# Five paddings that place float32r matmul operands 128 bytes apart modulo 256

## The chip, the cores and the metric

The kernel runs on one core of a Trainium2 chip. The metric is the device time of one launch in microseconds (us), lower is better. Tiles live in SBUF, the on-chip memory of 128 partitions; an address here is a byte offset within a partition. Matmuls run on TensorE (PE): the stationary operand is loaded by a weight load (PEld) and the moving operand streams past it into PSUM, the accumulation memory. The other engines are VectorE (DVE), ScalarE (ACT), GpSimd (POOL) and SyncE (SP), which issues the DMA transfers.

## The reference

Two blocks follow each other on 256 tokens of width 1024, all in float32. Cut to what matters here:

```python
# first block: layer 0 = window attention + S5 scan (with a GLU), layer 1 = attention over selected keys
for layer in range(2):
    hn = rms_norm(h, norm_g[layer])
    h = h + (even_layer if layer == 0 else odd_layer)(hn, ...)   # products with w_in, w_out, glu_w
# second block: layer 0 = attention, layer 1 = chunked SSM, both with 256 context tokens
for i in range(2):
    h, hc = modulate(x, ...), modulate(ctx, ...)
    y, yc = attention_mixer(h, hc, ...) if i == 0 else ssm_mixer(h, hc, ...)
    x = x + g1 * y
    x = x + g2 * swiglu(modulate(x, ...), w_gate[i], w_up[i], w_down[i])   # width 2816
    # the context gets the same in layer 0
return rmsnorm(x, final_norm_g)
```

Most of the work are products of 256 tokens with weight matrices: 1024 x 2304, 1024 x 3144, 1024 x 1536, 1024 x 6208, the three feed-forward matrices of each layer, and the output products.

## The kernel before

**Products.** Each weight tile of 128 x 1024 is fetched by one DMA into `raw`; `Weights.load` (L173) has ACT write its rounded copy `h` as float32r (L179) and DVE the remainder `l` (L180). Activations are split in the same way into a high and a low tile (`nhx` and `nlx`, `fh` and `fl`, `yH` and `yL` and so on). A product is the sum of three float32r matmuls: high by high, low by high, high by low. All go through the helper `mm` (L129), so all have line L130; in the profile `out<-moving,stationary` names their tiles. There are two forms:

- `feat_tiles` (L273) has the weights stationary and the activations moving, 256 columns. The output has features on partitions. Feed-forward gate and up (`pffnx`, `pffnc`), the SSM's projections (`pcvx`), gates (`pg`), the GLU (`pglu`) and others use it: for every k first `h` with the high and with the low activation, then, after all k, `l` with the high one.
- `tok_step` (L231) has the activations stationary (128 tokens) and the weights moving, 256 or 512 columns. The output has tokens on partitions (`pdx` for x, `pdc` for the context).

Every matmul has a weight load of its own, also where the stationary operand is the same as before. The weight load for the next matmul runs while the present one streams.

**Order.** The program is traced by a scheduler; the x chain and the context chain share TensorE. The last stages are x alone: the SSM's output product (stationary `ysH`, `ysL`), then the feed-forward of layer 1 in two halves of 11 column tiles, each with its product back to width 1024.

**Addresses.** Pools on the left are stacked upwards from the bottom of the partition in the order in which they are opened, those with `right=True` downwards from the top; a tile lies right behind the one before it. Left: `con` (constants, first tile `pad`, L110), `res`, `act` (split activations), `wk`, `xw`, then the stages' own pools (`ev`, `evat`, `od`, `l0`, `ff0`, `l1`, `ff1`). Right: `padr` (L189), `wx` (x weights), `wc` (context weights, L191), `cx` (context tiles, L192). Tiles that hold matmul operands have sizes that are multiples of 256 bytes, as have the slices of 128, 256 or 512 columns that a matmul takes, so each keeps one residue modulo 256: `h` and `l` of both weight pools 192; everything in `act` 0; `fh` and `fl` 0, in `cx` and in `ff0` and `ff1`; the GLU's `glH`, `glL` 192; `QxT`, `KxH`, `KxL` (L1220 and L1221) 0; `ysH`, `ysL` 128. The other places of the change are `sink` (L596, in `evat`, ahead of `glH` and `glL`) and `d_row` (L1332, in `l1`, ahead of `ysH` and `ysL`).

Of the kernel before, what the change touches and what calls it, by code (L numbers as in the profile page):

```python
# [8 lines left out]
F32 = mybir.dt.float32  # L9
# [79 lines left out]
def build(tc, A):  # L89
# [5 lines left out]
    def D(name):  # L95
        return A[name]

    def dram(a, off, ap):
        return bass.AP(tensor=a.tensor, offset=a.offset + off, ap=ap)

    def pool(name, bufs=1, space=None, right=False):
        kw = {"side": "right"} if right else {}
        if space is not None:
            kw["space"] = space
        else:
            kw["reuse_waits"] = "tile"
        return tc.tile_pool(name=name, bufs=bufs, **kw)

    con = es.enter_context(pool("con"))
    con.tile([128, 8], F32, name="pad")  # L110
    res = es.enter_context(pool("res"))
    act = es.enter_context(pool("act"))
    wk = es.enter_context(pool("wk", 2))
# [15 lines left out]
    def mm(out, l, r, start, stop, mark=None):  # L129
        i = T.matmul(out, l, r, start=start, stop=stop)  # L130
        if mark is not None:
            marks.setdefault(mark, i.ins)
# [55 lines left out]
    cst = ExitStack()  # L188
    es.enter_context(pool("pr", right=True)).tile([128, 8], F32, name="padr")  # L189
    wx = Weights("x", *WX, SY, es)  # L190
    wc = Weights("c", *WC, SY, cst)  # L191
    cx = cst.enter_context(pool("cx", right=True))  # L192
    xw = es.enter_context(pool("xw"))
    xpool = {"x": (xw, "xn"), "c": (cx, "cfl")}
# [31 lines left out]
    def w_plain(a, ncols):  # L226
        def src(k0, nk, n0, n):
            return [(lambda t: t, dram(a, k0 * 128 * ncols + n0, [[ncols, 128], [128 * ncols, nk], [1, n]]))]
        return src
# [16 lines left out]
    def dense_tok(w, src, actk, kt, chunks, evac, ps, tags="ddd", last=None):  # L246
        for ci, (n0, n) in enumerate(chunks):
            pt = [ps.tile([128, 512], F32, tag=tags[ci], name=f"pd{ps.k}{m}") for m in range(2)]
            kstep = 1024 // n
            for k0 in range(0, kt, kstep):  # L250
                ks = range(k0, min(k0 + kstep, kt))
                wh, wl = w.load(src(k0, len(ks), n0, n), len(ks), n)
                tok_step(pt, wh, wl, ks, n, actk, kt, last if ci == len(chunks) - 1 else None)
            for m in range(2):
                evac(ci, m, pt[m][:, :n], n0)
# [176 lines left out]
    def even_layer(hook):  # L432
        with ExitStack() as st:
            p = st.enter_context(pool("ev"))
# [6 lines left out]
            uT = p.tile([128, 4, 256], F32, name="uT")  # L441
            QT = p.tile([128, 4, 256], F32, name="QT")
            KT = p.tile([128, 256], F32, name="KT")
            Vt = p.tile([128, 2, 128], F32, name="Vt")
            sgb = p.tile([128, 4, 256], F32, name="sgb")
            sga = p.tile([128, 4, 256], F32, name="sga")
            at = st.enter_context(pool("evat"))
# [118 lines left out]
            def q_evac(ci, m, pq, n0):  # L566
                qn = p.tile([128, 4, 2, 64], F32, tag="qn", bufs=1)
                if ci == 0:
                    head_norm(p, pq, 8, 64, qn.rearrange("p g a d -> p a g d"), "e")
                    pt = psx.tile([128, 4, 128], F32, tag="m", name="pqt")  # L570
                    for g in range(4):
                        T.transpose(pt[:, g], qn[:, g].rearrange("p a d -> p (a d)"), flip)
                    S.activation(QT[:, :, m * 128:(m + 1) * 128], pt, AF.Identity, scale=g_q)
                else:
# [4 lines left out]
                    T.transpose(pt[:, 0], kn.rearrange("p a d -> p (a d)"), ident)  # L579
                    S.activation(KT[:, m * 128:(m + 1) * 128], pt[:, 0], AF.Identity, scale=g_k)  # L580

# [11 lines left out]
            sl = ssm.enter_context(pool("ssl"))  # L593
            yH = act.tile([128, 8, 256], F32R, tag="hx", name="yH")
            yL = act.tile([128, 8, 256], F32R, tag="lx", name="yL")
            sink = at.tile([128, 16], F32, name="sink")[:, 0:8]  # L596
            SY.dma_start(sink, dram(D("ev_sinks"), 0, [[0, 128], [1, 8]]))

            def attention(m):
# [4 lines left out]
                for a in range(2):  # L604
# [3 lines left out]
                    for g0 in range(0, 4, per):  # L608
                        lg = psx.tile([128, per, n], F32, tag="d", name="plg")
                        for g in range(per):  # L610
                            mm(lg[:, g], QT[r, g0 + g, ms], KT[r, 0:n], True, True)
                        V.scalar_tensor_tensor(Tt[:, g0:g0 + per], lg, 0.125, Tt[:, g0:g0 + per],
# [128 lines left out]
    def odd_layer(sc_b):  # L741
        with ExitStack() as st:
# [55 lines left out]

            QT = p.tile([128, 8, 256], F32, name="QTo")
            KT = p.tile([128, 2, 256], F32, name="KTo")  # L800
            Vt = p.tile([128, 2, 256], F32, name="Vto")

            def q_evac(ci, m, pq, n0):
# [7 lines left out]
                if ci < 2:  # L811
                    S.activation(QT[:, 4 * ci:4 * ci + 4, ms], pt, AF.Identity, scale=g_oq)
                else:
                    S.activation(KT[:, :, ms], pt[:, 0:2], AF.Identity, scale=g_ok)
                    V.tensor_copy(Vt[:, m], pq[:, 256:512])
# [8 lines left out]
            for a in range(2):  # L824
                Tz = p.tile([128, 4, 384], F32, tag="Tzo", name="Tzo")
                load_bias(Tz, sc_b, 1, 4 * a)
                for t in (1, 0):
# [4 lines left out]
                    for g0 in range(0, 4, per):  # L832
                        pl = psx.tile([128, per, n], F32, tag="m", name="plo")
                        for g in range(per):
                            mm(pl[:, g], QT[:, 4 * a + g0 + g, qs], KT[:, a, 0:n], True, False)
                            mm(pl[:, g], flip_b, sel[t], False, True)
# [96 lines left out]
    def gate_row(p, i, v, w, tag):  # L933
        t = p.tile([128, 1024], F32, tag=tag)
        SY.dma_start(t, dram(mod_rows[i][1], v * 6144 + w * 1024, [[0, 128], [1, 1024]]))
        return t

    def add_gated(xs, grow, key, last=True, apart=0):
        hold = [None]

        def f(ci, m, ps_, n0):
            n = ps_.shape[1]
            sl = slice(n0, n0 + n)
            if n0 % 512 == 0 or not apart:
                hold[0] = xpool[key][0].tile([128, 512], F32, tag="nt" + key, name="ag")
            z = n0 % 512 if apart else 0
            t = hold[0][:, z:z + n]
            V.tensor_tensor(t[:, :n], ps_, grow[:, sl], op=ALU.mult)
            V.tensor_tensor(xs[m][:, sl], xs[m][:, sl], t[:, :n], op=ALU.add)
            if last:  # L950
                square_sum(key, m, n0, xs[m][:, sl], t if apart else ps_)
            if "g" in final:
                V.tensor_tensor(final["o"][:, m, sl], xs[m][:, sl], final["g"][:, sl], op=ALU.mult)
        return f
# [101 lines left out]
    def keys_in(QT, KT, ks, t):  # L1056
        KH, KL = KT
        for e in range(2):
            a, b = rows_of(e), rows_of(1 - e)
            S.activation(KH[a, :, e, ks], t[a], AF.Copy)  # L1060
            S.activation(KH[b, :, e, ks], t[a], AF.Copy)
            V.tensor_tensor(KL[a, :, e, ks], t[a], KH[a, :, e, ks].bitcast(F32), op=ALU.subtract)
            V.tensor_tensor(KL[b, :, e, ks], t[a], KH[a, :, e, ks].bitcast(F32), op=ALU.subtract)
# [142 lines left out]
    def x_attention():  # L1206
        with ExitStack() as st:
            p = st.enter_context(pool("l0"))
            mt = mod[0]
            grow = gate_row(p, 0, 0, 2, "grow")  # L1210
            rope = p.tile([128, 2, 2, 64], F32, name="rope")
            SY.dma_start(rope, D("c_rope").rearrange("(m p) (z f) -> p m z f", p=128, z=2))
            mask = []
            for mk in (m_ge, m_le):
                t = p.tile([128, 128], BF16, name=f"wm{len(mask)}")
                V.tensor_scalar(t, mk, -1.0, 1e30, op0=ALU.add, op1=ALU.mult)
                mask.append(t)
            actk = norm_T(xt, mt[:, 0, 1], mt[:, 0, 0], "x", psx)
            wx.on_pool = LP[2]
            QT = p.tile([128, 2, 2, 4, 256], F32R, name="QxT")  # L1220
            KT = (p.tile([128, 2, 2, 512], F32R, name="KxH"), p.tile([128, 2, 2, 512], F32R, name="KxL"))  # L1221
            keys_in(QT, KT, slice(0, 256), KcT)
            Vt = p.tile([128, 2, 256], F32, name="Vx")
            dense_tok(wx, w_plain(w_qkv, 1536), actk, 8, ((1024, 512), (0, 512), (512, 512)),
                      lambda ci, m, pq, n0: qkv_evac(p, QT, KT, Vt, rope, psx, "x")((2, 0, 1)[ci], m, pq, n0), psx)
            oH = act.tile([128, 8, 256], F32R, tag="hx", name="oHx")
            oL = act.tile([128, 8, 256], F32R, tag="lx", name="oLx")
            vals = [Vc[:, 0], Vc[:, 1], Vt[:, 0], Vt[:, 1]]
            P2 = [p.tile([128, 2, 2, 512], F32, name="P2"), xw.tile([128, 2, 2, 512], F32, tag="xn", name="P3")]
            for m in range(2):  # L1230
                keys = [(KT, 0, None), (KT, 1, None), (KT, 0, None if m == 0 else mask[1]),
                        (KT, 1, None if m == 1 else mask[0])]
                attend(P2, p, QT, keys, vals, m, oH, oL, "x", (psx, "m"), (psx, "d"), (psc, "m"))
            dense_tok(wx, wo_attn, lambda k: (oH[:, k], oL[:, k]), 8, OUTC,
                      add_gated(xt, grow, "x"), psx, last="endo")
# [91 lines left out]
    def x_ssm():  # L1327
        with ExitStack() as st:
            p = st.enter_context(pool("l1"))
            mt = mod[1]  # L1330
            grow = gate_row(p, 1, 0, 2, "grow")
            d_row = p.tile([128, 32], F32, name="d_row")  # L1332
            SY.dma_start(d_row, dram(D("ssm_D_2"), 0, [[0, 128], [1, 32]]))
            actk = norm_T(xt, mt[:, 0, 1], mt[:, 0, 0], "x", psx, warm=("endx011", 4))
            wx.on_pool = LP[5]
# [219 lines left out]
```

## Time and profile before

| | us |
|---|---|
| median of 3 runs | 1568.02 |
| lowest and highest run | 1564.76, 1572.22 |
| the profiled execution | 1570.59 |
| its span, first to last instruction | 1568.8 |
| TensorE busy in it | 1494.5 |
| DVE busy | 1087.5 |
| ACT busy | 793.7 |

The profile is one execution. Its span is what the views divide up; the device time of the same execution is 1.8 us longer. The page gives busy times, the chain of work that ended last, and groups of instructions; the trace behind it can be asked for windows, single instructions and waits. A matmul's duration in it is longer than the distance to the next matmul, since matmuls overlap in the pipeline: the distance, here called the pitch, is a stretch's time divided by its count.

### The profile page before, as it was taken

The page shows a single profiled execution, that of the slowest core. Times are in us where ns is not written, and L with a number is a line of the kernel's source. Part 1 is how long each engine was busy: PE and PEld are TensorE (multiplying, and loading weights), DVE is VectorE, ACT ScalarE, POOL GpSimd, SP SyncE. Part 2 cuts the span into 40 slices and gives each one's busy share as a digit, 9 for nine tenths or more (in the row PEclk, how much of TensorE's full clock was granted, in tenths as well). Part 3 has the DMA queues.
Part 4 walks back from the last instruction along what each step waited for, and adds up shares of the span by engine and source line. Part 5 has one row for each costly group of instructions (what it writes and reads, how often), then busy time and mean ns, then how long its engine had stood idle before and what let it go on. Part 6 is the DMA issues. An engine that isn't in the chain of part 4 may idle for free.

```text
span 1568.8 us, 27033 instructions
## 1 busy us (share of the span) xinstructions
PE 1494.5 (95%) x10552; PEld 1269.3 (81%) x10552; DVE 1087.5 (69%) x1825; ACT 793.7 (51%) x1498; POOL 264.9 (17%) x227
## 2 busy tenths in 40 slices
PE   7799998999999999999999999997899999999998
PEld 5575545787788888678879999797899998699997
DVE  6579986667767677666565676667877876665666
ACT  4433345754446455667444544456656644354444
POOL 1535650001100100000000000018634500200000
PEclk9899999999999999999999999999999999999999
DMA  8774555456865666553576566544444433455664
GB/s 250 264 220 124 178 163 159 133 147 189 255 196 165 220 210 168 161 164 101 174 236 206 167 178 184 164 125 131 125 119 113 126 87 134 147 159 186 193 188 135
DMA packets 306176, 264.57 MB, mean 169 GB/s; under 512 B 27442, under 2 KB 260704, under 8 KB 306049
## 3 DMA queue, kind: packets, MB, share of 16 engines
q1 hardware_dynamic: 306048, 262.85, 55.8%
q8 instruction: 83, 1.36, 0.4%
q14 instruction: 45, 0.36, 0.1%
HBM read 261.47 MB, written 1.34 MB: 168 GB/s over the span
## 4 chain that ended last, share of the span: by engine, by line
PE 76%; DVE 9%; DMA 7%; ACT 3%; POOL 3%; issue 2%; SPq 1%; POOLq 0%; ACTq 0%; DVEq 0%
PE pdx L130 22%; PE pffnx L130 16%; PE pffnc L130 7%; PE pdc L130 6%; PE pcvx L130 5%; PE pg L130 3%; PE pada L907 2%; DVE l L180 2%; DMA araw<-ada_w 2%; DMA raw<-ev_w_in 2%; PE py L130 1%; DVE m L676 1%; PE pocx L130 1%; PE ptcx L1125 1%; ACT h L179 1%
## 5 line engine op out<-in xcount | busy, mean ns | idle before, releaser
L180 DVE TENSOR_TENSOR l<-raw,h 128x1024 fp32r<-128x1024 f32 (+2 forms) x370 | 456.5, 1234 | 269.6 <-ACT h L179 225.0
L179 ACT ACTIVATE h<-raw 128x1024 fp32r<-128x1024 f32 (+2 forms) x374 | 389.5, 1042 | 421.4 <-PE pdx L130 118.2
L130 PE MATMUL pffnx<-nlx,h 128*128 128x256 f32 x704 | 170.3, 281 | 0.6 <-DVE nlx L357 0.6
L130 PE MATMUL pffnx<-nhx,h 128*128 128x256 f32 x704 | 170.1, 280 | 0.0
L311 POOL TENSOR_TENSOR sums<-sums,nhalf 128x1 f32<-128x1 f32 x20 | 13.3, 670 | 746.0 <-DVE sums L307 735.9
L130 PEld LDWEIGHTS pffnx<-nlx,h 128*128 128x128 f32 x704 | 133.2, 189 | 2.6 <-issue 1.2
L130 PEld LDWEIGHTS pffnx<-nhx,h 128*128 128x128 f32 x704 | 133.2, 189 | 0.8 <-issue 0.8
L130 PE MATMUL pffnx<-nhx,l 128*128 128x256 f32 x704 | 97.5, 280 | 0.0
L130 PE MATMUL pdx<-h,nhx 128*128 128x256 f32 (+1 forms) x256 | 86.3, 354 | 5.4 <-DVE cv L1297 2.9
L130 PEld LDWEIGHTS pffnx<-nhx,l 128*128 128x128 f32 x704 | 88.9, 188 | 1.2 <-issue 1.2
L130 PE MATMUL pffnc<-nhc,h 128*128 128x256 f32 x352 | 89.4, 287 | 0.1
L130 PE MATMUL pffnc<-nlc,h 128*128 128x256 f32 x352 | 88.3, 284 | 0.3 <-DVE nlc L357 0.3
L130 PE MATMUL pdx<-h,nlx 128*128 128x256 f32 (+1 forms) x256 | 84.3, 347 | 0.0
L907 PE MATMUL pada<-araw,cT 128*32 128x256 f32 x704 | 68.8, 395 | 9.4 <-DMA araw<-ada_w 8.9
L130 PE MATMUL pdx<-h,fh 128*128 128x256 f32 (+1 forms) x264 | 76.9, 318 | 0.0
L130 PE MATMUL pdx<-h,fl 128*128 128x256 f32 (+1 forms) x264 | 76.6, 316 | 0.0
L130 PE MATMUL pcvx<-nhx,h 128*128 128x256 f32 x256 | 75.3, 303 | 0.0
L130 PE MATMUL pcvx<-nlx,h 128*128 128x256 f32 x256 | 70.6, 284 | 0.0
L130 PEld LDWEIGHTS pffnc<-nhc,h 128*128 128x128 f32 x352 | 66.2, 188 | 4.2 <-issue 2.6
L130 PEld LDWEIGHTS pffnc<-nlc,h 128*128 128x128 f32 x352 | 66.3, 188 | 2.3 <-issue 1.2
L130 PEld LDWEIGHTS pdx<-h,nhx 128*128 128x128 f32 x256 | 51.6, 202 | 12.3 <-issue 3.8
L130 PE MATMUL pdx<-l,nhx 128*128 128x256 f32 (+1 forms) x256 | 60.0, 348 | 0.5 <-DVE l L180 0.5
(605 smaller groups left out, 3808.5 us busy)
## 6 DMA issues: line engine op xcount, KB each, us to landing
araw<-ada_w SPq DMA_DIRECT2D x88, 512.0 KB
raw<-ffn_w_gate SPq DMA_DIRECT2D x66, 512.0 KB
raw<-ffn_w_up SPq DMA_DIRECT2D x66, 512.0 KB
raw<-ffn_w_down SPq DMA_DIRECT2D x54, 512.0 KB
raw<-ssm_w_in SPq DMA_DIRECT2D x48, 512.0 KB
raw<-od_w_in SPq DMA_DIRECT2D x25, 512.0 KB
raw<-attn_w_qkv SPq DMA_DIRECT2D x24, 512.0 KB
raw<-attn_w_o SPq DMA_DIRECT2D x32, 256.0 KB
```

The lines of the kernel that those rows point to most:

```text
L130: i = T.matmul(out, l, r, start=start, stop=stop)
L179: S.activation(h[:, :n], raw[:, :n], AF.Copy)
L180: (G if self.on_pool > 0 else V).tensor_tensor(l[:, :n], raw[:, :n], h[:, :n].bitcast(F32), op=ALU.subtract)
L311: G.tensor_tensor(s[:, 3:4], s[:, j - 1:j], nhalf[:, 0:1], op=ALU.pow)
L676: V.tensor_tensor_scan(m1[:, ri], mg, m1[:, ri], 0.0, op0=ALU.mult, op1=ALU.add)
L907: T.matmul(pt[32 * q:32 * q + 32, 0:256], cT[:, k, :], raw[:, q * 256:(q + 1) * 256], start=k == 0, stop=k == 7, tile_position=(0, 32 * q))
L1125: T.transpose(pt[:, e, r], P[:, e, r, ki * 128:(ki + 1) * 128], ident)
```

## The change

Two tiles that nothing but their own first columns is read of become larger, the first padding becomes larger, and two new paddings are made:

```diff
     con = es.enter_context(pool("con"))
-    con.tile([128, 8], F32, name="pad")
+    con.tile([128, 24], F32, name="pad")
...
     wx = Weights("x", *WX, SY, es)
     wc = Weights("c", *WC, SY, cst)
+    cst.enter_context(pool("pc", right=True)).tile([128, 48], F32, name="padc")
     cx = cst.enter_context(pool("cx", right=True))
...
-            sink = at.tile([128, 16], F32, name="sink")[:, 0:8]
+            sink = at.tile([128, 32], F32, name="sink")[:, 0:8]
...
             QT = p.tile([128, 2, 2, 4, 256], F32R, name="QxT")
+            p.tile([128, 32], F32, name="padk")
             KT = (p.tile([128, 2, 2, 512], F32R, name="KxH"), p.tile([128, 2, 2, 512], F32R, name="KxL"))
...
-            d_row = p.tile([128, 32], F32, name="d_row")
+            d_row = p.tile([128, 64], F32, name="d_row")[:, 0:32]
```

`pad` grows by 64 bytes, so all left pools move up by 64. `padc` takes 192 bytes between `wc` and `cx`, so the tiles of `cx` move down by 192. `sink` grows by 64, `d_row` by 128, `padk` takes 128 between `QxT` and `KxH`. The weight tiles stay where they are. The instructions stay as they are but for the addresses.

## Rows read from the trace of the kernel before

**Rows 1.** The page: span, chain by engine and by line, groups of weight splitting.
```profile
span 1568.8 us, 27033 instructions
...
PE 76%; DVE 9%; DMA 7%; ACT 3%; POOL 3%; issue 2%; SPq 1%; POOLq 0%; ACTq 0%; DVEq 0%
PE pdx L130 22%; PE pffnx L130 16%; PE pffnc L130 7%; PE pdc L130 6%; PE pcvx L130 5%; PE pg L130 3%; PE pada L907 2%; DVE l L180 2%; DMA araw<-ada_w 2%; DMA raw<-ev_w_in 2%; PE py L130 1%; DVE m L676 1%; PE pocx L130 1%; PE ptcx L1125 1%; ACT h L179 1%
...
L180 DVE TENSOR_TENSOR l<-raw,h 128x1024 fp32r<-128x1024 f32 (+2 forms) x370 | 456.5, 1234 | 269.6 <-ACT h L179 225.0
L179 ACT ACTIVATE h<-raw 128x1024 fp32r<-128x1024 f32 (+2 forms) x374 | 389.5, 1042 | 421.4 <-PE pdx L130 118.2
```

**Rows 2.** Groups of TensorE by shape: out, inputs, shape, count, busy us, mean ns.
```profile
L130 PE MATMUL pffnx<-nhx,h 128*128 128x256 f32 x704 | 170.1, 280 | 0.0
L130 PE MATMUL pffnc<-nhc,h 128*128 128x256 f32 x352 | 89.4, 287 | 0.1
L130 PE MATMUL pcvx<-nhx,h 128*128 128x256 f32 x256 | 75.3, 303 | 0.0
L130 PE MATMUL pcvx<-nhc,h 128*128 128x256 f32 x192 | 54.9, 286 | 0.0
L130 PE MATMUL pdx<-h,fh 128*128 128x256 f32 x176 | 42.0, 279 | 0.0
L130 PE MATMUL pdx<-h,nhx 128*128 128x512 f32 x112 | 45.5, 409 | 2.4 <-ACT h L179 2.4
L130 PE MATMUL pdx<-h,ysH 128*128 128x512 f32 x64 | 25.5, 403 | 0.1
```

**Rows 3.** Windows, L130's matmuls alone: from:to, us, busy us (count), clock, DMA.
```profile
87.00:95.00 8.00, 8.00 (x73) 1.00 0.98 256
334.00:347.00 13.00, 13.00 (x113) 1.00 0.54 152
925.00:975.00 50.00, 50.00 (x427) 1.00 0.64 185
1018.00:1024.00 6.00, 6.00 (x53) 1.00 0.00 0
993.00:1006.00 13.00, 13.00 (x117) 1.00 0.64 182
1385.00:1435.00 50.00, 50.00 (x444) 1.00 0.65 191
1475.00:1525.00 50.00, 50.00 (x427) 1.00 0.64 186
```

**Rows 4.** The chain in order of time: start us, us, what, count.
```profile
913.65 7.71 PE pffnx L130 x68
922.62 54.26 PE pffnx L130 x460
...
1348.53 14.22 PE pdx L130 x62
...
1375.94 61.78 PE pffnx L130 x527
1437.72 30.94 PE pdx L130 x198
1468.66 62.19 PE pffnx L130 x528
1530.85 29.48 PE pdx L130 x190
```

**Rows 5.** Timeline of TensorE in the GLU: start us, us, instruction; 13 starts apart.
```profile
267.08 0.28 PE L130 MATMUL pglu<-glH,h 128*128 128x256 f32 x1
...
268.64 0.28 PE L130 MATMUL pglu<-glL,h 128*128 128x256 f32 x1
```

**Rows 6.** Timeline of TensorE where the moving operand is bf16, and what follows.
```profile
438.99 0.27 PE L130 MATMUL plo<-sel,flip_b 128*128 128x256 bf16 x1
439.10 0.60 PE L130 MATMUL plo<-KTo,QTo 128*128 128x256 f32 x2
439.54 0.27 PE L130 MATMUL plo<-sel,flip_b 128*128 128x256 bf16 x1
439.64 0.60 PE L130 MATMUL plo<-KTo,QTo 128*128 128x256 f32 x2
```

**Rows 7.** The longest of TensorE's waits: waiting line, releaser, us in total, times, longest.
```profile
PE pada L907 <- DMA araw<-ada_w: 8.9, 8, 2.2
```

## The prediction

> **What bounds the kernel now.** I read the page first. TensorE is busy for 95% of the span and is 76% of the chain that ended last, and five lines of the chain, all float32r matmuls, make 22, 16, 7, 6 and 5% of the span; `pg` adds 3% [rows 1]. That is 59%, some 930 us of 1568.8. The busy share alone says little, because a matmul's recorded duration (280 ns) overlaps the next one's; what counts is the distance from one start to the next, the pitch. Waits are no large part: the longest that the table of waits has for TensorE is 8.9 us in total [rows 7]. So a change of the pitch goes almost wholly to the end.
>
> The pitch comes from the chain's long pieces, where TensorE waits for nothing: time divided by count. 460 matmuls of 256 columns took 54.26 us, 118.0 ns each, and 528 took 62.19 us, 117.8 ns; but 68 with the same line and the same tiles took 7.71 us, 113.4 ns [rows 4]. The windows show it side by side: 50 us hold 427 matmuls in two stretches and 444 in a third, all at the full granted clock (2.4 GHz) [rows 3]. (A count includes the two or three that began before the window.) So float32r matmuls of 256 columns have two levels, 113.3 and 117.8 ns, and a stretch keeps its level until something interrupts it. 256 columns at 2.4 GHz are 106.7 ns by division, so both levels carry an extra cost, of 6.7 and 11.1 ns. Where the moving operand is bf16, also 256 columns, the next matmul starts 0.10 or 0.11 us later [rows 6]: the small extra of the float32r ones isn't in that row.
>
> For 512 columns the chain gives sums. The piece of 198 matmuls holds 66 of 512 columns and 132 of 256; with 132 at 117.8 ns the 66 have 233.3 ns each: (30.94 - 15.55) / 66. The piece of 190 gives the same with 113.3 ns for its 124 short ones [rows 4]. But the 62 in a row of the SSM's output product took 14.22 us, 229.4 ns [rows 4]. Those have the same moving tile `h` (192 modulo 256 bytes) and the same shape; their stationary `ysH`, `ysL` lies at 128, that of the others at 0. And in the GLU, where both operands lie at 192, 13 matmuls of 256 columns take 1.56 us, 120.0 ns [rows 5]. So the pitch does depend on the two addresses.
>
> **The change part by part.** No instruction, wait, DMA or byte of data is added or taken away: five tiles are made, or made larger, that nothing reads, and what lies behind them moves by 64 to 192 bytes. Worked out from the tiles' order and sizes, moving and next stationary operand lie as follows, modulo 256. (a) Products with features on partitions: activations 0 and weights 192 before; 64 and 192 after. (b) Token products: weights 192 and activations 0 before, 192 and 64 after. (c) The GLU: 192 and 192 before, 64 and 192 after. (d) Queries and keys of the x attention: 0 and 0 before, 192 and 64 after. (e) The SSM's output product: 192 and 128 before, 192 and 64 after. So the distance was 64 in (a), (b) and (e), none in (c) and (d), and becomes 128 in all. No row of before shows a dense run at 128; it has to be bounded.
>
> The nearest rows: at distance 0 120.0 ns, at 64 either 117.8 or 113.3 ns; for 512 columns 233.3 or 229.4 ns at 64, by the side on which the stationary lies. The cost falls as the two get further apart, and 128 is the furthest. I take for 256 columns that all runs have the lower level, 113.3 ns, and for 512 columns 229 ns, the lowest that rows show. The bounds are on one side no extra cost at all, the bf16 row's pitch of about 109 ns, and on the other the GLU's 120.0 ns.
>
> The counts: the shapes listed [rows 2] come in threes (h with the high part, h with the low part, l with the high part); with the 24 smaller groups of the same view they make 6,887 matmuls of 256 columns and 1,324 of 512. The share at the upper level I estimate from windows: 13 + 50 + 6 + 50 us of those shown are at it, and 8 + 13 + 50 us at the lower [rows 3], 63%; the projections (`pcvx`, 1,344) were at it wherever I looked, so I take 70%. Then 256 columns save 6,887 x 0.70 x 4.44 ns = 21.4 us. Of the 1,324, 192 have 229 ns already; the others save 1,132 x 4.4 ns = 5.0 us. Together 26.4 us of matmul time.
>
> On the path: the six lines have 930 us of the chain; all these matmuls at their pitch are 6,887 x 116.4 + 1,324 x 232.7 ns, some 1,110 us. So 84% lie on it: 22.2 us. Of that I give a tenth back, an estimate: 7% of the chain is DMA and 3% ACT [rows 1], and a weight tile that landed just in time will then be waited for. DVE's and ACT's 1.23 and 1.04 us for a weight tile [rows 1] stay well under the 2.7 us that 24 matmuls take. That leaves 20 us.
>
> The other edits cost nothing that I can show: DVE, ACT and DMA get tiles that lie 64 bytes further on. They stay on multiples of 64; the weight tiles, which carry most bytes, don't move at all. If a tenth of the DMA part of the chain for `araw` (2%, some 31 us [rows 1]) were lost or won by it, that is 3 us either way; I take 0. Plain float32 matmuls are not what the paddings aim at, and I leave them at what they take.
>
> Against the idea stands a rule. Rows 4 and 5 show pitches that differ with the stationary operand's address alone. The Trainium skill (SBUF — State Buffer, Who interferes with whom) gives TensorE two independent read ports, one for the moving operand and one for the weight load, and says that TensorE never waits on anyone; by it the addresses could not matter, and the sum would be 0. The 229.4 against 233.3 ns at one shape speak against it, but it is the page's form of the first rival. The same skill (TensorE: Matmul & The Clock Gate, Back-to-back issue gap) gives N / 2.4 + 2.5 ns, from which I estimate 109.2 and 215.8 ns for 256 and 512 columns; the bf16 row agrees for the first, and no row here shows the second.
>
> **The rivals.** *No change.* The two levels exist at one and the same pair of addresses (the stretches from 925 and from 1385 us [rows 3]), so the level is set by how the two streams happen to start, not by the distance, and the shares stay. Against it: the 512-column rows and the GLU. It gives 1568 us, and 3 us either way.
> *All of the extra goes.* If at 128 the two reads never meet, 256 columns take some 109 ns and 512 some 220: 6,887 x 7.2 + 1,324 x 12.7 ns = 66 us, 56 on the path, 50 after the tenth: 1518 us. For it: the bf16 row. Against it: no float32r run is below 113.3 ns, which is 272 cycles, 17 for each 16 columns, and that looks like a rate of the moving stream itself.
> *Slower.* The moving stream reads twice as many bytes in a matmul as the weight load does, so it overtakes the load's address, and what counts may be where it overtakes; then 128 can be as bad as 0. Price: the GLU's 120.0 ns for all 256-column matmuls, 6,887 x 3.6 = 24.8 us, and 233.3 for the 192 long ones, 0.8 us; 84% of it is 21 us: 1589 us. It decides where the mean pitch at 128 lies above today's 116.4 ns.
>
> **How the numbers follow.** The profiled execution took 1570.59 us around a span of 1568.8 us; less 20 it is 1550.6. The median of the three runs is 1568.0, 2.6 below that execution, so I predict 1548; its own range is 1538 to 1558 (half to one and a half times the gain). Chances: the forecast 0.43, all of the extra gone 0.14, no change 0.23, slower 0.20. The range that should hold 8 in 10 takes in the first three, 1513 to 1576. Half a per cent, 8 us, is about what a measurement of this kernel can tell from no change. Faster by more than that: 0.43 + 0.14 and nothing of the others, 0.57; within it 0.24, of which 0.01 is from the slow case; slower 0.19.
>
> **What would show it.** In the last feed-forward (the chain's pieces of 527 and 528) each piece at the full clock should be near 113.3 ns a matmul, none at 117.8; the long token products at 229 ns or under; the GLU at 113 instead of 120; the projections at 113 instead of 117.8. Counts, busy time of DVE and ACT, bytes and waits should stay. I am wrong if the two levels persist, if a new level above 118 ns appears, or if the pitch falls and the chain gets as much more DMA or DVE time as it loses of TensorE's.

## The result, and the profile after

The change makes the kernel slower: 1581.9 us, median of 7 runs (1574.98 to 1583.1), against 1568.44 us for 7 runs of the kernel before (1564.76 to 1572.57). The ratio is 1.0077, with a 95% interval of 1.0055 to 1.0099: 8.6 to 15.5 us more. The prediction was 1548 us, 20 us less; its range, 1513 to 1576, does not hold the time.

The page after has as many instructions, the same busy time of DVE's and ACT's weight splitting and nearly the same chain by line [rows 1]. What grew is PE: 78% of the chain instead of 76%, 1507.2 us busy instead of 1494.5.

```profile
span 1578.7 us, 27033 instructions
PE 1507.2 (95%) x10552; PEld 1282.1 (81%) x10552; DVE 1087.7 (69%) x1825; ACT 793.2 (50%) x1498; POOL 265.1 (17%) x227
PE 78%; DVE 8%; DMA 6%; POOL 3%; ACT 2%; issue 2%; SPq 1%; POOLq 0%; DVEq 0%; ACTq 0%
L180 DVE TENSOR_TENSOR l<-raw,h 128x1024 fp32r<-128x1024 f32 (+2 forms) x370 | 456.0, 1233 | 277.6 <-ACT h L179 233.9
L179 ACT ACTIVATE h<-raw 128x1024 fp32r<-128x1024 f32 (+2 forms) x374 | 389.5, 1043 | 431.3 <-PE pdx L130 121.1
```

The chain after in order of time (start, duration, what, count), the pieces that answer to [rows 4]:

```profile
919.56 8.07 PE pffnx L130 x68
928.89 54.66 PE pffnx L130 x460
...
1355.34 14.43 PE pdx L130 x62
...
1446.45 31.00 PE pdx L130 x198
1477.45 62.65 PE pffnx L130 x528
1540.10 30.05 PE pdx L130 x190
```

Every piece is longer than its twin of before, and those that had been at the lower level most of all: 68 matmuls 8.07 us instead of 7.71; 460, at the upper level before, 54.66 instead of 54.26; 190 with 124 short ones 30.05 instead of 29.48. So the lower level went, and the upper one moved up too, to 118.7 ns.

The windows of 50 us in the two feed-forwards of x, L130's matmuls alone (from:to, us, busy us and count, the same for the weight loads, granted clock, DMA share, GB/s):

```profile
935.00:985.00 50.00, 50.00 (x417) 49.71 (x416) 1.00 0.62 188
1395.00:1445.00 50.00, 50.00 (x424) 50.00 (x423) 1.00 0.64 189
1485.00:1535.00 50.00, 50.00 (x424) 50.00 (x423) 1.00 0.63 182
```

Before, undisturbed windows of this length held 427 or 444 [rows 3]. Now they hold 424, and 444 is nowhere; the clock is 1.00, as before. (The first window takes in some longer matmuls of another tile.) The GLU's starts, 120.0 ns apart before [rows 5], are 118.2 ns apart, 2.60 us for 22, no lower than the rest:

```profile
265.80 0.28 PE L130 MATMUL pglu<-glL,h 128*128 128x256 f32 x1
...
268.40 0.28 PE L130 MATMUL pglu<-glH,l 128*128 128x256 f32 x1
```

TensorE's longest wait for a DMA hardly moved (8.9 us before [rows 7]):

```profile
PE pada L908 <- DMA araw<-ada_w: 8.6, 9, 2.2
```

So the loss is in the pitch. To add it up I took, from the trace, the time from each float32r matmul's start to the next one's where nothing was waited for and the full clock was granted, and averaged it by shape and by distance. Distance here means (next stationary operand - moving operand) modulo 256 bytes, with its sign, so 64 and 192 are the same gap on the two sides.

| group | matmuls | before: distance, ns | after: distance, ns | change, us |
|---|---|---|---|---|
| products with features, 256 columns | 5,010 | 192, 117.02 | 128, 118.81 | +9.0 |
| token products, 256 columns | 1,550 | 64, 115.47 | 128, 118.77 | +5.1 |
| token products, 512 columns | 978 | 64, 233.17 | 128, 232.26 | -0.9 |
| product of `ysH`, `ysL`, 512 columns | 184 | 192, 229.21 | 128, 232.26 | +0.6 |

(The counts leave out matmuls behind a wait, at the lower clock, or where the shape changes; in after the two 512-column groups lie at one distance and are averaged together.) That is 13.8 us of matmul time. The ratio of the medians gives 12.1 us of 1568.4; the two profiled executions, from which the sum comes, took 1570.59 and 1580.52 us, 9.9 us apart. Hence most of it arrived at the end.

### The profile page after: what moved, and what is told of

It reads as the page before. It is cut to its first block, busy times and chain, and to the rows that moved or that the text cites. A ratio compares the mean times of both kernels' runs of the same rounds, so it can differ in the third digit from the quotient of the medians.

```text
span 1578.7 us, 27033 instructions
## 1 busy us (share of the span) xinstructions
PE 1507.2 (95%) x10552; PEld 1282.1 (81%) x10552; DVE 1087.7 (69%) x1825; ACT 793.2 (50%) x1498; POOL 265.1 (17%) x227
## 4 chain that ended last, share of the span: by engine, by line
PE 78%; DVE 8%; DMA 6%; POOL 3%; ACT 2%; issue 2%; SPq 1%; POOLq 0%; DVEq 0%; ACTq 0%
PE pdx L130 22%; PE pffnx L130 16%; PE pffnc L130 8%; PE pdc L130 6%; PE pcvx L130 6%; PE pg L130 3%; PE pada L908 3%; DMA araw<-ada_w 2%; DMA raw<-ev_w_in 2%; DVE l L180 2%; PE py L130 1%; PE pocx L130 1%; DVE m L677 1%; PE ptcx L1126 1%; PE pqi L130 1%
## 5 line engine op out<-in xcount | busy, mean ns | idle before, releaser
L130 PE MATMUL pffnx<-nlx,h 128*128 128x256 f32 x704 | 172.0, 283 | 0.8 <-DVE nlx L358 0.8
L130 PE MATMUL pffnx<-nhx,h 128*128 128x256 f32 x704 | 171.9, 282 | 0.0
L130 PEld LDWEIGHTS pffnx<-nlx,h 128*128 128x128 f32 x704 | 132.5, 188 | 3.1 <-DVE nlx L358 1.3
L130 PEld LDWEIGHTS pffnx<-nhx,h 128*128 128x128 f32 x704 | 132.7, 188 | 0.8 <-issue 0.8
L130 PE MATMUL pffnx<-nhx,l 128*128 128x256 f32 x704 | 98.8, 282 | 0.0
L130 PE MATMUL pdx<-h,nhx 128*128 128x256 f32 (+1 forms) x256 | 86.7, 355 | 5.0 <-DVE cv L1299 2.6
L130 PEld LDWEIGHTS pffnx<-nhx,l 128*128 128x128 f32 x704 | 89.9, 188 | 1.2 <-issue 1.2
L130 PE MATMUL pffnc<-nhc,h 128*128 128x256 f32 x352 | 90.9, 290 | 0.0
L130 PE MATMUL pffnc<-nlc,h 128*128 128x256 f32 x352 | 89.6, 288 | 0.3 <-DVE nlc L358 0.3
L130 PE MATMUL pdx<-h,nlx 128*128 128x256 f32 (+1 forms) x256 | 84.3, 347 | 0.0
L130 PE MATMUL pdx<-h,fh 128*128 128x256 f32 (+1 forms) x264 | 78.1, 320 | 0.0
L130 PE MATMUL pdx<-h,fl 128*128 128x256 f32 (+1 forms) x264 | 77.9, 319 | 0.0
L130 PE MATMUL pcvx<-nhx,h 128*128 128x256 f32 x256 | 74.4, 299 | 0.2 <-DVE cv L1299 0.2
L130 PE MATMUL pcvx<-nlx,h 128*128 128x256 f32 x256 | 70.7, 285 | 0.0
L130 PEld LDWEIGHTS pffnc<-nhc,h 128*128 128x128 f32 x352 | 66.6, 189 | 4.1 <-issue 2.5
L130 PEld LDWEIGHTS pffnc<-nlc,h 128*128 128x128 f32 x352 | 66.7, 189 | 2.2 <-issue 1.2
L130 PEld LDWEIGHTS pdx<-h,nhx 128*128 128x128 f32 x256 | 51.5, 201 | 11.7 <-ACT h L179 3.5
L130 PE MATMUL pdx<-l,nhx 128*128 128x256 f32 (+1 forms) x256 | 59.6, 346 | 0.6 <-DVE l L180 0.6
```

## Experiments

Each expectation names its theories by letters of its own. All ratios are to the kernel before, run on the same chip.

**A map of the pitch by distance.** A kernel with matmuls alone: one moving tile, one stationary tile, dense runs of 40 (24 for 512 columns) at one distance each, and one short matmul between two runs. The loop of its helper `run`:

```python
for i in range(count):
    a = mo + (i % 4) * n
    b = so + (i % 4) * 128
    T.matmul(o[0:cols, :n], sta[:, b:b + cols], mov[:, a:a + n], start=i == 0, stop=i == count - 1)
```

> This kernel leaves the whole computation out: it loads x, rounds it to float32r, copies x to the output and runs only matmuls, in stretches of 40 (24 for 512 columns) with one moving and one stationary residue each, the distance (stationary of the next matmul less moving operand, modulo 256 bytes) going from 0 to 240 in steps of 16; each distance is started four times for 256 columns, twice for 512, after a separating matmul of another width. Theory D (the distance decides): for 256 columns 120.0 ns at distance 0, 113.3 or 117.8 at 64 and 192, 118.7 or 120.0 at 128; for 512 columns 233.3 at 64, 229.0 at 192, 232.5 at 128, whatever the absolute residues are. Theory S (how a stretch starts decides): every distance shows several levels, among them 113.3 at 128 and at 0, and the levels follow the separating matmul. Theory A (the moving operand's own residue decides: 64 or 192 after the change, 0 or 192 before): with the moving operand fixed, all distances give one pitch, and the stretches in which both are moved together differ.

Chain of this kernel in order of time (start, duration, tile, count): `sax` is distance 0, `sex` 64, `six` 128, `smx` 192, all of 256 columns; `lax` 0 and `lix` 128 of 512. A piece is 39 or 23 pitches and the rest of its last matmul.

```profile
36.47 4.86 PE sax L40 x40
...
104.16 4.61 PE sex L40 x40
...
181.44 4.81 PE six L40 x40
...
259.43 4.77 PE smx L40 x40
...
337.29 5.54 PE lax L40 x24
...
428.13 5.65 PE lix L40 x24
```

The starts from the ninth matmul on give the pitch itself:

| distance, bytes | 0 | 16 | 32 | 48 | 64 | 80 | 96 | 112 | 128 | 144 | 160 | 176 | 192 | 208 | 224 | 240 |
|---|---|---|---|---|---|---|---|---|---|---|---|---|---|---|---|---|
| 256 columns, ns | 120.0 | 118.3 and 120.0 | 118.4 | 117.8 | **113.3** | 118.7 and 119.9 | 117.3 and 118.7 | 120.0 | **118.7** | 120.0 | 120.1 | 118.1 | 117.8 | 116.7 | 116.7 | 120.0 |
| 512 columns, ns | **226.6** | 226.7 | 233.4 | 233.3 | 233.4 | 232.0 | 234.3 | 233.4 | **232.4** and 233.3 | 233.5 | 233.3 | 230.0 | 229.0 | 231.8 | 233.4 | 226.7 |

With both tiles moved on together by 64 or 128 bytes, distances 0, 64, 128 and 192 gave the same times within 0.4 ns, but for one of the two starts at 128, which gave 120.0. So of the residues the distance alone counted here, and the cost does not fall with it: 128 is among the dear ones, and what is cheapest for 256 columns is not so for 512. With 32 stationary columns instead of 128, a smaller weight load, 256 columns took 113.3 ns at 0, 64 and 192 and 115.6 at 128. With 64 they took 120.0, 119.2, 116.6 and 116.7 ns at 0, 64, 128 and 192. The dearer pitches are thus bound to the size of the load as well as to its place, but a smaller load is not always the cheaper one: at 64 bytes the load of 64 columns is dearer than that of 128, and for it 128 bytes is the cheapest of the four.

**All distances 0.** The kernel before with four paddings (`pad` 56, `padc` 16, `sink` 32, `d_row` 64), which put nearly all operands on residue 192:

```diff
-    con.tile([128, 8], F32, name="pad")
+    con.tile([128, 56], F32, name="pad")
...
+    cst.enter_context(pool("pc", right=True)).tile([128, 16], F32, name="padc")
```

> The kernel before with paddings that put moving and next stationary operand at the same residue, 192, in all products: distance 0. Theory D: the GLU's pitch everywhere, 120.0 ns for 256 columns instead of a mean of 116.6, so 6,887 x 3.4 = 23 us more, for 512 columns 233 instead of 229 for 192 of them, 1 us; 1568 + 24 x 0.95 = 1591 us. Theory S: the two levels of before in some mixture, 1568 us, 4 either way.

1582.22 us, ratio 1.0077 [1.0055, 1.0100]. The chain's pieces of 460 and 528 read

```profile
930.72 55.27 PE pffnx L130 x460
...
1482.01 63.36 PE pffnx L130 x528
```

that is 120.0 ns a matmul. The 512-column token products, which I had left at 233.3, came to 229.06 on average and 226.7 in the long runs, as the map says. Together 5,010 x 2.72 + 1,550 x 4.27 - 978 x 4.11 ns = +16.2 us; the medians are 12.1 us apart, the profiled executions (1570.59 and 1585.6 us) 15.0. Theory D's 1591 us was 9 too high, 4 of them by the 512 columns; the distance, not theory S's mixture of the old levels, set the pitch.

**The two signs exchanged** (the run swap). `pad` 40, `padc` 32, `sink` 32, `d_row` 64: products with features at 64, token products at 192.

> The kernel before with paddings that exchange the two distances: feature products 64 instead of 192, token products 192 instead of 64, the SSM's output product at 192 as before. Theory D: 256 columns stay at 113.3 or 117.8 ns, the long token products fall from 233.3 to 229.0 ns, 1,130 x 4.3 = 4.9 us less; 1568 - 4 = 1564 us, a ratio of 0.997. Theory S: no change but for the share of the levels, 1568 us, 4 either way.

1566.29 us, ratio 0.9978 [0.9963, 0.9993], so a little faster than the kernel before. Products with features 115.55 ns on average (117.02 before), 256-column token products 116.86 (115.47), 512-column ones 230.27 (233.17; 230.27 is the mean of both 512-column groups, which here lie at the same distance, 192). Both levels are still there: the run of matmuls after 1369 us was at 113.3, the piece of 528 after 1461 us at 117.8:

```profile
1369.06 62.25 PE pffnx L130 x527
1431.32 30.07 PE pdx L130 x198
1461.38 62.19 PE pffnx L130 x528
1523.57 30.02 PE pdx L130 x190
```

The first piece is no shorter than the third because its first matmuls ran at a granted clock of 0.50, that is 1.2 GHz, as those of its twin of before did; windows of L130 at its start:

```profile
1371.00:1373.00 2.00, 2.00 (x11) 2.00 (x11) 0.50 0.35 106
1373.00:1376.00 3.00, 3.00 (x25) 3.00 (x24) 0.85 0.30 104
```

**The change in two parts.** First `pad` alone, with `sink` 64 and `d_row` 80, which keep the other operands where they were:

```diff
-    con.tile([128, 8], F32, name="pad")
+    con.tile([128, 24], F32, name="pad")
```

> The kernel before with the larger first padding alone (pad of 24 columns, the other four places moved back by as much, so that cx, the GLU, the x attention and ysH, ysL lie as before). The products with features (5,010 matmuls of 256 columns, distance 192 -> 128) and most token products (1,309 of 256 columns and 856 of 512, distance 64 -> 128) are as in the kernel after. Theory S (the distance sets the pitch; 118.8 against 117.0 and 115.5 ns, 232.3 against 233.2 ns): 8.9 + 4.4 - 0.8 = 12.5 us of matmul time, 84 to 100% of it on the path: 1579 to 1581 us, ratio 1.007 to 1.008. Rival P (the paddings cost through other tiles: the context's tiles in cx, the context's DMA and DVE work): 1568 us here, ratio 1.000 to 1.002, and the loss in the run of the other four.

1578.05 us, 1.0056 [1.0038, 1.0073]: 6.0 to 11.4 us more. 118.92 ns in the products with features, 118.74 in the token products that moved. Its pieces are those of the kernel after:

```profile
914.65 8.07 PE pffnx L130 x68
923.98 54.66 PE pffnx L130 x460
...
1349.92 14.21 PE pdx L130 x62
```

The third, `ysH` and `ysL`, stayed at 192 here and has before's 14.2 us, not after's 14.43. Then the other four places alone:

```diff
+    cst.enter_context(pool("pc", right=True)).tile([128, 48], F32, name="padc")
...
+            p.tile([128, 32], F32, name="padk")
```

> The other four edits alone (padc of 48 columns, padk, sink and d_row; pad as before). Distance 128 only for the context's feed-forward product (241 matmuls of 256 columns and 122 of 512), ysH and ysL (184 of 512), the x attention's queries and keys (85) and the GLU (97, from 0). Theory S: 241 x 3.3 + 184 x 3.1 - 122 x 0.9 - 97 x 1.2 ns = +1.1 us: 1568 to 1570 us, ratio 1.000 to 1.001. Rival P (the loss comes by cx and its padding): 1579 to 1582 us, ratio 1.007 to 1.009.

1570.83 us, 1.0007 [0.9985, 1.0028]: no difference. Its `ysH` piece is after's, its pieces of 68 and 460 are before's:

```profile
918.55 7.71 PE pffnx L130 x68
927.52 54.26 PE pffnx L130 x460
...
1350.48 14.43 PE pdx L130 x62
```

The loss is thus in the first padding, by the products whose distance it makes 128, and not in the tiles of the context.

**What chooses between the two levels.** Runs of matmuls alone again, each behind another kind of interruption, and runs without one in between.

> Matmuls alone on one and the same data, nothing of the reference is computed; the time itself says nothing. Dense float32r runs of 30 matmuls of 256 columns at distance 64 and at 192, each behind another kind of interruption: one matmul of 64, 72, 128, 256 or 512 columns, one or two plain float32 matmuls, one, two or three bf16 matmuls, a wait for ScalarE of a short, a middle and a long time; then runs that follow each other without any interruption at changing distances. Theory A (how a dense run starts decides between its two levels, 113.3 and 117.8 ns): behind some kinds distance 64 gives 117.8 and distance 192 gives 113.3, the reverse of what they gave behind the matmuls of 64 to 120 columns so far; and runs without an interruption carry a state on, so that what one distance gives depends on the run before. Theory B (the distance alone decides, and the two levels in the full kernel have another cause, such as other engines' traffic): distance 64 gives 113.3 and 192 gives 117.8 behind every kind and in every order.

Theory A holds in the main: both levels occur at both signs. Distance 64 gave 113.3 behind most interruptions and 117.8, among others, behind those meant as the longest wait for ScalarE (`kmxe`, both times); 192 gave 117.8 behind most and 113.3 behind those (`kmxm`, both times). But TensorE did not wait there: the scheduler put the dense runs ahead of the matmul that waits for ScalarE, and the table of TensorE's waits has one entry, ahead of all runs:

```profile
PE warm L40 <- ACT sta L32: 9.2, 1, 9.2
```

What stood ahead of those runs were one or two matmuls of 256 columns in an unbroken stream. What a wait does to the level is thus not shown.

Where 30 matmuls of 256 columns follow another 30 without an interruption, the state is carried on over a change of sign (`qe`, `rb`, `rf`, `rh` at 192; `qf`, `ra`, `rc`, `re`, `ri` at 64):

```profile
229.63 3.53 PE qex L40 x30
233.16 3.40 PE qfx L40 x30
...
289.16 3.49 PE rax L40 x30
292.64 3.40 PE rbx L40 x30
296.05 3.54 PE rcx L40 x30
...
303.12 3.54 PE rex L40 x30
306.65 3.53 PE rfx L40 x30
...
313.72 3.54 PE rhx L40 x30
317.25 3.40 PE rix L40 x30
```

A row of 3.40 us is at 113.3 ns a matmul, one of 3.53 or 3.54 at 117.8; `ra`, behind a short matmul, begins with one of 0.20 us and is at 113.3 from its fourth on. From 192 to 64 (`qe` to `qf`, `rb` to `rc`, `rh` to `ri`) the level changes each time, from 64 to 192 (`ra` to `rb`, `re` to `rf`) it stays. The full kernels do the same where their chain is unbroken: the last four pieces of before lie at 192, 64, 192, 64 and are at the lower, upper, upper, lower level [rows 4]; with the signs exchanged they lie at 64, 192, 64, 192 and are at the lower, lower, upper, upper level (the chain above). So there is a state beside the distance, and one product hands it on to the next. At 128 the one run between two others (`qk`) took 118.65 ns, at 0 (`qm`) 120.0.

> Matmuls alone, nothing of the reference is computed; the time itself says nothing. First, runs of 40 matmuls of 256 columns in which the distance of a matmul's moving operand to its own stationary operand differs from the distance to the next one's: own 0 and next 128; own 128 and next 0; own 0 and next 64 and 192 in turn; own 64 and 192 in turn and next 0. Theory N (what meets is the present moving stream and the next matmul's weight load): the next one's distance decides, so 118.7, 120.0, between 113.3 and 117.8, 120.0 ns. Theory O (a matmul's own two operands meet): 120.0, 118.7, 120.0, between 113.3 and 117.8 ns. Then dense runs of 24 behind 24 waits for ScalarE of as many different lengths, at distance 64 and 192, and behind 8 at 128 and at 0. Theory R (the start picks one of two states, each start anew): both 113.3 and 117.8 ns occur at 64 and at 192, some of each among 24; at 128 118.7 or 120.0 and nothing below; at 0 120.0 alone. Theory F (one of the two is the rule and the other needs a special neighbour): one level in nearly all of the 24.

Here too TensorE waited in none of the dense runs; what stands between two stretches are single matmuls of 256 columns:

```profile
92.45 2.72 PE wex L40 x24
95.17 0.12 PE sep L84
95.29 0.23 PE wex L40 x2
95.64 2.83 PE wex L40 x24
```

At 64 the first stretch is at 113.3 ns and the 20 behind it are at 117.8; at 192 18 are at 117.8 and 4 at 113.3; at 128 five lie near 118.8 and three at 120.0 or just above; 0 gave 120.0. These are not separate starts, as the expectation meant them, but pieces of one stream: the 20 at 64 show a level that is kept across such matmuls, not how often a start picks it. Theories R and F stay open. The first part, in which own and next distance differ, fell between the two theories: own 0 with next 128, and own 128 with next 0, both 116.7 ns; own 64 and 192 with next 0, 116.7 once and 120.0 twice; own 192 with next 64, 116.7, which is neither of the two levels. The distance to the next stationary operand alone doesn't decide then, nor that to a matmul's own; here the moving operands also alternate between two residues, as in no product of the kernel. Which reads meet is left open.

**Setting the state.** In the map every run behind a short matmul started low at distance 64, so I put one short matmul, whose result is overwritten (the run nudge2), ahead of every second tile of the products with features in the kernel with exchanged signs:

```diff
         wh, wl = w.load(parts, kt, 128)
+        marks["nudge"] = marks.get("nudge", 0) + 1
+        if marks["nudge"] % 2 == 0:
+            ah, out = uses[0][0](0)[0], uses[0][1]
+            mm(out[:, 0:64], ah[:, 0:128], ah[:, 0:64], True, True)
```

> The kernel of the run swap (products with features at distance 64, token products at 192) with one more matmul of 64 columns, whose result is overwritten, ahead of every second tile of the products with features, 91 in all. Theory N (a short matmul within a dense stream makes the runs behind it start in the lower state at distance 64, as it did in nearly all runs of matmuls alone, while waits leave them in the upper one): the products with features come from 115.6 to 113.5 ns, 5,010 x 2.1 = 10.5 us less; 91 extra matmuls at 40 to 60 ns cost 4 to 5 us; 5 us net on the path: 1561 us, ratio to the kernel before 0.995, and no run longer than 48 at 117.8. Theory R (each start picks a state anew, by nothing that a short matmul sets): mean pitch stays at 115.6 and the extra matmuls cost: 1570 us, ratio 1.001.

1563.03 us, 0.9962 [0.9944, 0.9980], faster than the kernel before. All runs of 46 behind a short matmul in the products with features were at 113.3 ns, and so were the token products that follow the feed-forwards of x, with 228.9 for their 512 columns; the mean of the products with features is 114.62 (115.55 in the run swap), not the 113.5 of theory N. But a short matmul costs 0.14 us, not the 40 to 60 ns that I had put: 48 matmuls and one short one took the 5.58 us between these two rows of TensorE's timeline, against 48 x 0.1133.

```profile
1480.50 0.19 PE L130 MATMUL pffnx<-nhx 128*128 128x64 f32 x1
...
1486.08 0.19 PE L130 MATMUL pffnx<-nhx 128*128 128x64 f32 x1
```

At that price the 91 cost 12.7 us, more than the 7 or so that the pitches save against the run swap; by this sum nudge2 should be the slower of the two. The times don't show it either way: their intervals overlap. Theory N's remark that waits leave the runs in the upper level rests on the matmuls alone, where, as said, there was no wait.

With fewer of them, ahead of every fourth, eighth and twenty-second tile:

> As the run nudge2, but ahead of every fourth tile, 45 extra matmuls. Theory N: mean pitch of the products with features 113.5 to 114.0 ns, 8 us less, 2 us for the extra matmuls, 5 us net: 1561 us, ratio 0.995. Theory R: 115.6 ns as before, 1568 us, ratio 1.000.

1567.15 us, 0.9985 [0.9972, 0.9998], 114.65 ns: theory N's time and pitch were both missed. Here the scheduler also ordered the x and the context chains otherwise in the middle: TensorE reaches the tile `plo` 15 us later than in before's trace and the end of the first half of x's first feed-forward 2 us earlier, so this run says little of the price.

> As the run nudge2, but ahead of every eighth tile, 23 extra matmuls; in nudge2 each cost 0.14 us (48 matmuls and one short one from 1480.53 to 1486.11 us: 5.58 - 48 x 0.1133). Theory N (the state that a short matmul sets holds until a wait or another shape interrupts): the long runs of the two feed-forwards of x at 113.3 ns from the first short matmul on, mean of the products with features 114.7 to 115.2 ns, that is 9 to 11 us less than before, 3.5 us less in the 512-column products, 3 us for the extra matmuls: 9 to 11 us net, half to all of it at the end: 1559 to 1563 us, ratio 0.994 to 0.997. Theory H (the state is lost again within some tiles): mean 115.5 ns and 1566 us, ratio 0.998, as in the run swap.

1564.46 us, 0.9969 [0.9954, 0.9985], 114.76 ns. The time is a little above theory N's, the ratio and the pitch lie within it. Runs of 190 behind a short matmul stay at 113.3; theory H falls.

> As the run nudge8, but ahead of every twenty-second tile, 8 extra matmuls, 1 us. Theory N: between the runs swap and nudge8, mean of the products with features 115.0 to 115.5 ns: 1561 to 1566 us, ratio 0.995 to 0.998. Theory H: as swap, 115.5 ns, 0.998.

1566.77 us, 0.9987 [0.9975, 0.9999], 114.99 ns: the time is above both forecasts, the pitch at the lower end of theory N's. This one shows the effect best. In the second half of the last feed-forward 167 matmuls run at 117.8, then the short one comes, and the other 358 run at 113.3. Windows ahead of and behind it, with the columns as above, and the short matmul itself:

```profile
1468.00:1484.00 16.00, 16.00 (x138) 16.00 (x137) 1.00 0.68 196
1488.00:1504.00 16.00, 16.00 (x144) 16.00 (x143) 1.00 0.64 186
```
```profile
1486.18 0.20 PE L130 MATMUL pffnx<-nhx 128*128 128x64 f32 x1
```

The two addresses, the clock and the tiles are the same on both sides of it, and the DMA share changes by 0.04. The short matmul sets the lower level and does not merely change it: 90 us earlier a piece was at 113.3 ns already, and stayed there behind one (at 1395.4 us):

```profile
1380.00:1394.00 14.00, 14.00 (x126) 14.00 (x125) 1.00 0.59 172
1398.00:1412.00 14.00, 14.00 (x126) 14.00 (x125) 1.00 0.66 191
```

Not every short interruption does so: in the same run, and in the run swap, 12 matmuls of 32 columns (`pend`) stand between the pieces of x's first feed-forward, and it is at 117.8 ns on both sides of them; among the matmuls alone, one dense run at distance 64 behind a matmul of 64 columns (`kaxe`) was at 117.8 too. Nor is a gain in device time shown: the intervals of all four runs overlap that of the run swap, 0.9978 [0.9963, 0.9993].

## Why the prediction was wrong

**What bounds the kernel** held: the pitch of dense float32r matmuls. Where the paddings moved the mean pitch of the products with features (by 1.5 to 2.7 ns: the change, `pad` alone, all distances 0, the signs exchanged), the time went the same way; where they left it (the other four places alone), the time stayed. TensorE's longest wait hardly changed (8.9 us before, 8.6 after).

**The step that failed** is "the cost falls as the two get further apart, and 128 is the furthest". It was drawn through three values, 120.0 at distance 0 and two values at 64 [rows 4, 5], as if the cost were a slope. The map shows no slope: 120.0, 113.3, 118.7, 117.8 at 0, 64, 128, 192. I had also written that no row of before shows a dense run at 128, and yet took for the forecast the lowest value that rows show at other distances. Instead of 4.44 ns less in 70% of 6,887 matmuls, the 6,560 of the two large groups got 1.8 or 3.3 ns dearer. That is most of the error: +14.1 us where -21.4 stood.

**Two levels at one pair of addresses** were in the rows, and the forecast took it that the lower one would be had everywhere. The levels 113.3 and 117.8 belong to the gap of 64 on either side. Which of them a product gets is not its own matter: in the feed-forwards of x it is handed on from the product ahead. Before, this gave the token product the other level than the product with features ahead of it, so one of the two was always dear; the forecast had no such step. At 128 there are two as well, but 118.7 and 120.0; the change did not make the lower state safe, it left the two distances, of the four multiples of 64, that have it.

**The 512-column term** had 4.4 ns less in 1,132 matmuls, 5.0 us. The 978 long token products got 0.9 ns cheaper, the 184 of `ysH` and `ysL` 3.1 dearer: 0.3 us in all. The inference from 229.4 and 233.3 that the side matters was right in part: at 64 all dense runs had 233.3, but at 192 there were both 228.9 and 233.3 (run swap, with the level of the matmuls around them), and at 128 the pitch lies between.

**The counts and the path.** The counts held. The share of 84% on the path fits: 12.1 of 13.8 us by the medians, with an interval of 8.6 to 15.5, and 9.9 by the two executions from which the sums come. Exchanging the signs took 5,010 x 1.47 + 978 x 2.90 - 1,550 x 1.39 - 184 x 1.06 ns = 7.9 us of matmul time; the medians fell by 3.4 us (1.1 to 5.8), the profiled executions (1570.59 and 1563.96 us) by 6.6. So the gain may have been smaller than the share says, or the level of the pieces differs from one execution to the next; the runs do not tell these apart, and the tenth that I gave back was not tested by itself.

**The rivals.** "Slower" was right in its sign, in its place and in the point from which it decides (mean pitch above 116.4 ns; it became 118.8), and its price was too high, 21 us against 12, because it took 120.0 ns for 128. Its reason, a moving stream that overtakes the load, was not tried. "No change" was right that a state of the two streams at their start sets the level, and wrong that the distance has no part in it: all four kernels with other paddings moved as their distances do. "All of the extra goes" has nothing for it; no float32r run of 256 columns was below 113.3.

**The rule weighed.** By the Trainium skill (SBUF — State Buffer, Who interferes with whom) the two reads are independent and the addresses could not matter. The kernel with all distances 0 and the one with `pad` alone have the same instructions as before and are 12.1 and 8.8 us slower, with 119.7 and 118.9 ns on average in the products with features. The measurement decides. Of the rows that I set against the rule, only rows 4 differ in the stationary operand's address alone; in the GLU [rows 5] it is the moving operand that lies elsewhere, at 192 instead of 0.

**Signs named beforehand.** Of those, "a new level above 118 ns" came true: 118.7.

## What to carry to other kernels

Two levels of one matmul's pitch at one pair of addresses say that a state decides beside the addresses, and it may have been set several products earlier; an edit of addresses should then be priced by a run of the very distance that it makes, and a kernel with matmuls alone gives the whole table in one run. For dense float32r matmuls of 128 x 128 stationary and 256 moving columns, a next stationary operand 64 bytes ahead of the moving one, modulo 256, was the best of those measured, 128 and 0 the worst of the multiples of 64; 512 columns had their best at 0, and a load of 64 columns had another order. One short matmul can turn a long run from the upper level to the lower; at 0.14 us for it and 4.4 ns saved a matmul, an estimate from these runs is that it pays from some 32 matmuls on, but no device time here shows the gain.

## What was not expected of the hardware

- Four of the pitches are multiples of 16 cycles at 2.4 GHz: 113.3, 120.0, 226.7 and 233.3 ns are 272, 288, 544 and 560 cycles, 17, 18, 34 and 35 times 16. The levels 117.8 and 118.7 are means over a repeating pattern: single pitches read 117 to 119 ns in groups of three and 115 to 122 in groups of five, and three or five together are 848 and 1,424 cycles, 53 and 89 times 16.
- 512 columns at distance 0 take 226.7 ns, where 256 columns take 120.0, about the longest that they take anywhere.
- A dense run kept its level, over 527 matmuls in the longest, and handed it on to the next product, through 66 matmuls of 512 columns too: the same level from distance 64 to 192, the other from 192 to 64. One matmul of 64 columns changed 117.8 to 113.3 ns in mid-stream.
- Why a short matmul sets the state, what a wait does to it, and which reads meet, is not settled.
